# Dividing PSUM into three large and two small tiles in an encoder-layer kernel

## The chip, the cores and the metric

The kernel runs on one core of a Trainium2 chip. The metric is the device time of one execution in microseconds (us), taken as the median of several runs. Where a time is split up below, it comes from one profiled execution of the program.

## The reference

One layer of a bidirectional encoder is computed for two groups of tokens with the same weights: a group of 1024 tokens ("prompt") and one of 512 ("sample"), each with 256 memory tokens, at a model width of 1024, in float32. Cut to what matters:

```python
h = rms_norm(x, ln_pre)
z = h @ w_in            # 1024 -> 6400: inputs, gates and merge logits of all branches
pool_out  = multiscale_pool(pool_in, w_pool, pool_scale)     # 4 groups, windows 2, 4, 8, 16
attn_out  = self_attention(rope(norm(q)), rope(norm(k)), v)  # 8 heads of 64, 2 key heads
cross_out = cross_attention(xq, rms_norm(mem), w_mem_kv)     # 4 heads of 128, 256 memory tokens
branches  = pool_out * silu(pool_gate), attn_out * silu(attn_gate), cross_out * silu(x_gate)
merged    = sum(sigmoid(merge_logits[n] + b_merge[n]) * (branches[n] @ w_branch[n]) for n in range(3))
y         = x + rms_norm(merged @ w_out, ln_post)
```

## The kernel before

**Tiles.** Matrix products are made in parts: each operand is split into a high part and a low rest in the fp32r format (`split`, L164), and `mm3` (L132) adds three matmuls high x high, high x low and low x high in one PSUM sum. PSUM has eight banks of 512 float32 numbers in each of 128 partitions. Two helpers hand out all of it: `A()` (L91) gives a tile of 1024 numbers (two banks), of which there are two, and `B()` (L94) a tile of 512 (one bank), of which there are four. A tile that is asked for while all of its kind are in use is waited for: the first instruction that writes it waits for the last reader of the tile that had the place before. In SBUF there are, among others, eight half-wide buffers `HU()` (L85), three buffers `RAW()` for weights as loaded (L88), and two pairs for split weights (L168).

**Order of the work.** The program is written as Python generators that issue instructions stage by stage. The framework then orders the instructions of each engine by their place in the program, with some moved ahead (`tc.high_priority`, with EVAC = 200 for readers of PSUM) and by when the buffers that they need come free; so the order on each engine belongs to this program, and another division of buffers gives another order. Each engine runs its queue in order. All DMAs are issued from one queue, that of SyncE (SP).

**Stages.** (1) About 0 to 83 us: `mem_phase` (L660) makes keys and values of the memory tokens, and `long_h` (L232) normalises the group of 1024. It holds it as two by two blocks (features 0 to 511 and 512 to 1023 by tokens 0 to 511 and 512 to 1023). For each half of the tokens, `spread` (L209) brings the factors of the norm into a PSUM tile by a product with ones, and `scaled` (L254) multiplies the input by them.

(2) About 83 to 590 us: `products` (L318) makes the projections of the long group in pairs of 128 output channels. For each pair a two by two block product is made from seven block products in place of eight (Strassen's scheme in Winograd's form): the weights' sums are made on VectorE (L331 to L334), those of the input once in `long_h`. The seven products, 12 matmuls each, are added into three sums X, Y and Z in the order X Y X Z X Z X (L363), each in a B. Between them the sums are read: products 0, 2 and 3 are copied out by ScalarE (`keep`, L355 to L358), and products 1, 4 and 5 are added to such a copy by VectorE (`both`, L360, by `summed`, L416); the last is taken as it is. So X is read and written on four times, Z twice and Y once. There are 25 pairs. After each product a background task may run a step: the tails `kv_tail` (L567), `q_tail` (L595) and `pool_tail` (L622), which take an A for transposes (the first two) and Bs for small transposes or products.

(3) About 590 to 690 us: `plain` (L393) makes the first projections of the short group as ordinary products, 24 matmuls each into a B, with tails in the background (L1104).

(4) About 690 to 1150 us: attention. `stream` (L888) runs units of one head and 128 queries: `scores` (L771) makes scores in an A, takes the maximum (L782), the exponential (L784) and the division; `turn` (L789) transposes the result into another A and splits it (L165 and L162); `values` (L802) multiplies it with the values into a B that serves two units and is read by `gated` (L874, L882 and L883). `weave` (L108) puts between these the rest of the short group's projections (`plain` again, L1106), each in a B that L463 and L464 or L479 read. The cross-attention and the short group's attention follow in the same stream.

(5) From about 1150 us, for each of three blocks of 512 tokens: `branches` (L966) and `merge` (L981) make 24 merge products of 12 matmuls, each into a B that L996 multiplies with a loaded gate (`sg`, L988); then `out_phase` (L1003) makes the output in two halves. The first half uses two As (L1030, L1031), the second two Bs and an A. Their readers are L1026 and L1027; `finish` (L1011) makes the norm and the residual sum (L1020), and the store. In the last block the second half is cut up, with a further A (L1046) and `ending` (L1063).

Of the kernel before, what the change touches and what calls it, by code (L numbers as in the profile page):

```python
# [14 lines left out]
ALU = mybir.AluOpType  # L15
# [3 lines left out]
P = 128  # L19
D = 1024  # L20
KC = D // P
BLK = 512
# [39 lines left out]
def encoder_kernel(ctx: ExitStack, tc, wt, xs, xts, mt, cols, rows, rope, edge, ys):  # L62
    nc = tc.nc
    v, act, pool, pe = nc.vector, nc.scalar, nc.gpsimd, nc.tensor
# [4 lines left out]
    ps = ctx.enter_context(tc.tile_pool(name="ps", bufs=1, space=bass.MemoryType.PSUM))  # L69
# [5 lines left out]
    def nm(s):  # L75
        count[0] += 1
        return f"{s}_{count[0]}"
# [7 lines left out]
    def HU(dt=F32):  # L85
        return sb.tile([P, BLK], dt, tag="hu", bufs=NHU, name=nm("hu"))

    def RAW():  # L88
        return sb.tile([P, D], F32, tag="raw", bufs=NRAW, name=nm("raw"))

    def A(dt=F32):  # L91
        return ps.tile([P, 1024], dt, tag="A", bufs=2, name=nm("A"))

    def B(dt=F32):  # L94
        return ps.tile([P, 512], dt, tag="B", bufs=4, name=nm("B"))

    def S(n):
        return st.tile([P, n], F32, tag=f"s{n}", bufs=3 if n == 16 else 8, name=nm("s"))
# [5 lines left out]
    def run(g):  # L104
        for _ in g:
            pass
# [31 lines left out]
    def load(out, src):  # L138
        return nc.sync.dma_start(out, src)  # L139

    colt = const.tile([P, 44], F32, name="colt")
# [32 lines left out]
    def weights(*key, pieces=1):  # L174

        raw = RAW()
        load(raw[:], wt[TILES[key]])
        hi, lo = WT()
        with tc.high_priority(AHEAD):
            for i in range(pieces):  # L180
                s = slice(i * D // pieces, (i + 1) * D // pieces)
                split(hi[:, s], lo[:, s], raw[:, s])
        return lambda s: (hi[:, s], lo[:, s])
# [25 lines left out]
    def spread(r, out=None):  # L209

        dg = U()[:, :BLK]
        shape = [P, TT, P]
        v.tensor_tensor(dg.rearrange("p (t m) -> p t m", t=TT), ident[:].unsqueeze(1).broadcast_to(shape),
                        r.unsqueeze(2).broadcast_to(shape), op=ALU.mult)
        b = B()
        cost[0] += 3 * BLK / 2.4
        mm(b[:], ones[:], dg, start=True, stop=True)
        if out is None:
            return b[:]
        with tc.high_priority(EVAC):  # L220
            act.activation(out, b[:], AF.Copy)
# [10 lines left out]
    def long_h(xt, h):  # L232

        h += [[None] * 4 for _ in range(7)]
        xv = xt.rearrange("p (k t) -> p k t", k=KC)
        q = [[M(F32) for _ in range(2)] for _ in range(2)]
        for j in range(2):
            for i in range(2):
                load(q[i][j][:].rearrange("p (c n) -> p c n", c=4), xv[:, i * 4:i * 4 + 4, j * BLK:(j + 1) * BLK])
        yield  # L240
        r, sp, sq = S(16), [], []
        for j in range(2):
            sq.append([squares(q[i][j][:]) for i in range(2)])
            yield
        for j in range(2):
            rj = r[:, j * TT:(j + 1) * TT]
            mean_squares(sq[j], rj)
            rstd_of(rj)
            yield
            sp.append(spread(rj))  # L250
            yield
        b11, b12, b21, b22 = [[q[i][j][:, :D], q[i][j][:, D:]] for i in range(2) for j in range(2)]

        def scaled(i, j):  # L254
            for c in range(4):
                x = q[i][j][:, c * BLK:(c + 1) * BLK]
                v.scalar_tensor_tensor(x, x, colt[:, i * 4 + c:i * 4 + c + 1], sp[j], op0=ALU.mult, op1=ALU.mult)

        def put(k, x):
            for c in range(2):  # L260
                parts_of(h[k], 2 * c, x[c])

        def difference(out, a, b):
            for c in range(2):
                v.tensor_tensor(out[c], a[c], b[c], op=ALU.subtract)

        scaled(0, 0)
        put(0, b11)
        yield
        scaled(1, 0)  # L270
        put(1, b21)
        yield
        scaled(0, 1)
        scaled(1, 1)
        yield
        t3, t4 = (U(), U()), (U(), U())
        difference(t3, b22, b12)
        difference(b12, b12, b11)
        difference(b11, b22, b12)
        put(2, b11)  # L280
        put(3, b12)
        put(4, t3)
        put(5, b22)
        difference(t4, b21, b11)
        put(6, t4)
# [32 lines left out]
    def products(pairs, h, n, background):  # L318

        ops = {}  # L320

        def prepare():
            for p, (k0, k1, _) in enumerate(pairs):
                r0, r1 = RAW(), RAW()
                load(r0[:], wt[TILES[k0]])
                load(r1[:], wt[TILES[k1]])
                a11, a12, a21, a22 = r0[:, :BLK], r0[:, BLK:], r1[:, :BLK], r1[:, BLK:]
                ta, tb = SUM(), SUM()
                s2, s1, s3, s4 = ta[:, :BLK], ta[:, BLK:], tb[:, :BLK], tb[:, BLK:]
                with tc.high_priority(AHEAD):  # L330
                    v.tensor_tensor(s1, a21, a22, op=ALU.add)  # L331
                    v.tensor_tensor(s2, s1, a11, op=ALU.subtract)
                    v.tensor_tensor(s3, a11, a21, op=ALU.subtract)
                    v.tensor_tensor(s4, a12, s2, op=ALU.subtract)  # L334
                for i, x in enumerate((r0[:], ta[:], tb[:], a22)):
                    hi, lo = [w[:, :x.free_size()] for w in WT()]
                    with tc.high_priority(AHEAD):
                        split(hi, lo, x)
                    for k in range(2 if i < 3 else 1):
                        ops[p, 2 * i + k] = [w[:, k * BLK:(k + 1) * BLK] for w in (hi, lo)]  # L340
                    yield

        prep = prepare()
        done = 0

        def ready(i):
            nonlocal done
            while done < i and next(prep, prep) is not prep:
                done += 1

        for p, (_, _, take) in enumerate(pairs):
            banks = {}
            kept = {}

            def keep(k, b):  # L355
                kept[k] = HU()
                with tc.high_priority(EVAC):
                    act.activation(kept[k][:, :n], b, AF.Copy)  # L358

            def both(i, j, b, k):  # L360
                take(i, j, b, kept.pop(k)[:, :n])

            for i, bank in enumerate("XYXZXZX"):  # L363
                ready(p * 4 + i // 2 + LOOK)
                start = bank not in banks
                if start:
                    banks[bank] = B()
                b = banks[bank][:, :n]
                w = ops.pop((p, i))
                for c in range(4):  # L370
                    s = slice(c * P, (c + 1) * P)
                    mm3(b, (w[0][:, s], w[1][:, s]), h[i][c], start and c == 0, c == 3,
                        skip_group_check=True)
                    if c == 1:
                        yield
                if i == 0:
                    keep("p1", b)
                elif i == 1:
                    both(0, 0, b, "p1")
                elif i == 2:  # L380
                    keep("p16", b)
                elif i == 3:
                    keep("p5", b)
                elif i == 4:
                    both(1, 1, b, "p5")
                elif i == 5:
                    both(0, 1, b, "p16")
                else:
                    take(1, 0, b, None)
                next(background, None)  # L390
                yield

    def plain(pairs, h, background):  # L393

        for k0, k1, take in pairs:
            for i, key in enumerate((k0, k1)):
                w, b = weights(*key), B()
                for k in range(KC):
                    mm3(b[:], w(slice(k * P, (k + 1) * P)), h[k], k == 0, k == KC - 1)
                    if k == 3:  # L400
                        next(background, None)
                        yield
                take(i, 0, b[:], None)
                next(background, None)
                yield

    def summed(b, s, out=None):

# [682 lines left out]
    h, hs = [], []  # L1091
# [5 lines left out]
    sc, kt, vt, pairs, bg, tasks, drained = group(1)  # L1097
# [3 lines left out]
    run(drained(products(pairs[-4:], h, BLK, bg)))  # L1101
    run(pre)
    scs, kts, vts, pairs, bg, _, drained = group(0)
    run(plain(pairs[0], hs, bg))  # L1104
    merged = []
    fill = drained(plain(pairs[1], hs, bg))  # L1106
    units = [u for b in range(2) for u in attention(b, sc, kt, vt)]
    units += [u for b in range(2) for u in cross(b, sc, mkd[1], mvd[1])]
    units += pairs_of(scs, kts, vts) + cross(0, scs, mkd[0], mvd[0])
# [103 lines left out]
```

## Time and profile before

| | us |
|---|---|
| median of three runs | 1500.23 (1493.72 to 2429.65) |
| the profiled execution | 1496.65 |
| its span, first to last instruction | 1494.8 |
| TensorE busy with matmuls | 1456.0 |
| VectorE busy | 976.5 |
| ScalarE busy | 709.6 |
| GpSimd busy | 273.3 |
| mean granted clock of TensorE | 0.989 |

The profile names engines PE (TensorE; PEld is its loading of weights, which overlaps), DVE (VectorE), ACT (ScalarE), POOL (GpSimd) and SP (SyncE, whose queue issues the DMAs). A row of the time line has its start and length in us, the engine, the line of the kernel, the operation, the tiles as out<-in, shapes, the number of merged instructions, and in brackets the idle time before and what ended it. A row of a stretch has its length, then the busy time and the number of instructions of PE, PEld, DVE, ACT and POOL, the granted clock as a share of full speed, the share of DMA time and GB/s. A row of waits has who waited for whom, the us in total, how often, and the longest. The ends of matmuls are modelled, so that a matmul that starts 0.23 us after the one before it is shown as 0.39 us long; starts are the better guide. "whi" and "wlo" are split weights, "med" the split inputs, so that B<-med,whi is a product into a small tile.

### The profile page before, as it was taken

The numbers are of one execution on the slowest core, as the hardware profiler recorded it, in microseconds if no ns is written. First come the engines' busy times: TensorE is split into PE (matmuls) and PEld (weight loads), VectorE is DVE, ScalarE is ACT, GpSimd is POOL, SyncE is SP. The second block draws the span as 40 slices with busy tenths as digits, with TensorE's granted clock in tenths as the row PEclk, the third lists the DMA queues.
The fourth block names the chain that finished last, engine by engine and source line by source line (L and its number), as shares of the span: only waits on it lengthen the run. The fifth ranks groups of instructions, "written<-read, shape, count | busy, mean of one in ns | idle before, by whom it ended". The sixth has DMA issues, their size and how long they took to land.

```text
span 1494.8 us, 19564 instructions
## 1 busy us (share of the span) xinstructions
PE 1456.0 (97%) x7264; PEld 1210.1 (81%) x7264; DVE 976.5 (65%) x1215; ACT 709.6 (47%) x1083; POOL 273.3 (18%) x286
## 2 busy tenths in 40 slices
PE   7979999999999999999999999999998999999998
PEld 5768888888888888887888888888886888888887
DVE  6996586666648564747767666676775664764764
ACT  6444444544434545434656556566675233323332
POOL 1000020110000000301222222234232150250241
PEclk9989999999999999999999999999999999999999
DMA  7513233332422434344222223165446844954952
GB/s 277 172 47 106 85 114 125 108 132 66 129 92 78 158 133 128 102 150 148 64 96 80 91 68 106 58 219 173 155 155 214 286 148 132 347 193 140 336 163 84
DMA packets 88174, 211.37 MB, mean 141 GB/s; under 512 B 9872, under 2 KB 19216, under 8 KB 87312
## 3 DMA queue, kind: packets, MB, share of 16 engines
q1 hardware_dynamic: 88080, 210.14, 42.7%
q8 instruction: 57, 0.93, 0.3%
q14 instruction: 37, 0.30, 0.1%
HBM read 155.57 MB, written 54.53 MB: 141 GB/s over the span
## 4 chain that ended last, share of the span: by engine, by line
PE 85%; DMA 4%; DVE 4%; ACT 4%; issue 2%; SPq 1%; POOL 0%; DVEq 0%; POOLq 0%; ACTq 0%
PE B L126 66%; PE A L126 14%; PE A L130 5%; ACT u L784 1%; DVE s L782 1%; ACT whi L165 1%; DMA raw<-wt 1%; DVE wlo L162 1%; PE B L130 1%; DMA hu<-xq 1%; ACT med L165 1%; SPq L139 1%; DMA u<-x_prompt 0%; DMA hu<-merge 0%; DMA hu<-x_gate 0%
## 5 line engine op out<-in xcount | busy, mean ns | idle before, releaser
L126 PE MATMUL B<-med,whi 128*128 128x512 f32 x2776 | 871.2, 394 | 15.8 <-ACT med L165 15.8
L126 PEld LDWEIGHTS B<-med,whi 128*128 128x128 f32 x2776 | 515.8, 189 | 122.2 <-ACT med L165 17.5
L126 PE MATMUL B<-med,wlo 128*128 128x512 f32 x1388 | 544.1, 392 | 0.6 <-DVE wlo L162 0.6
L126 PEld LDWEIGHTS B<-med,wlo 128*128 128x128 f32 x1388 | 261.9, 189 | 56.6 <-DVE wlo L162 1.7
L162 DVE TENSOR_TENSOR wlo<-raw,whi 128x1024 fp32r<-128x1024 f32 (+1 forms) x169 | 213.3, 1263 | 141.6 <-ACT whi L165 140.7
L165 ACT ACTIVATE whi<-raw 128x1024 fp32r<-128x1024 f32 (+1 forms) x169 | 167.5, 991 | 288.5 <-PE B L126 198.3
L165 ACT ACTIVATE med<-A 128x1024 fp32r<-128x1024 f32 x92 | 94.3, 1025 | 108.4 <-PE A L130 108.2
L162 DVE TENSOR_TENSOR med<-A,med 128x1024 fp32r<-128x1024 f32 (+1 forms) x93 | 113.0, 1215 | 42.0 <-ACT med L165 40.8
L187 POOL TENSOR_SCALAR s<-s 128x16 f32<-128x16 f32 (+3 forms) x17 | 6.9, 404 | 669.0 <-DVE s L556 333.2
L786 POOL TENSOR_SCALAR u<-u,s 128x1024 f32<-128x1024 f32 x64 | 72.1, 1127 | 251.3 <-DVE s L785 219.1
L130 PE MATMUL A<-ident,u 128*128 128x128 f32 x784 | 102.8, 273 | 0.9 <-DVE med L162 0.2
L130 PEld LDWEIGHTS A<-ident,u 128*128 128x128 f32 x784 | 90.1, 140 | 16.3 <-issue 5.2
L998 POOL TENSOR_TENSOR med<-med,hu 128x512 f32<-128x512 f32 x48 | 77.0, 1617 | 142.3 <-DVE hu L996 142.2
L782 DVE TENSOR_REDUCE s<-A 128x1 f32<-128x1024 f32 x64 | 78.1, 1220 | 32.9 <-PE A L126 11.3
L126 PE MATMUL A<-kt,med 128*128 128x512 f32 x320 | 91.9, 409 | 2.7 <-ACT u L784 1.2
L126 PE MATMUL A<-whi,med 128*128 128x512 f32 (+1 forms) x320 | 92.4, 368 | 0.2 <-ACT hu L1027 0.2
L784 ACT ACTIVATE u<-A,s 128x1024 f32<-128x1024 f32 x64 | 71.3, 1114 | 38.4 <-DVE s L782 38.0
L165 ACT ACTIVATE whi<-sum 128x1024 fp32r<-128x1024 f32 x50 | 53.1, 1062 | 65.6 <-PE B L126 63.7
L162 DVE TENSOR_TENSOR med<-med,med 128x1024 fp32r<-128x1024 f32 (+1 forms) x50 | 55.8, 1127 | 38.1 <-ACT med L165 34.2
L165 ACT ACTIVATE med<-med 128x1024 fp32r<-128x1024 f32 (+1 forms) x44 | 44.2, 1017 | 74.8 <-POOL med L998 36.2
L162 DVE TENSOR_TENSOR wlo<-sum,whi 128x1024 fp32r<-128x1024 f32 x50 | 61.1, 1221 | 23.3 <-ACT whi L165 22.4
L126 PE MATMUL B<-med,vt 128*128 128x256 f32 x512 | 75.9, 287 | 0.4 <-ACT med L165 0.4
(179 smaller groups left out, 1610.4 us busy)
## 6 DMA issues: line engine op xcount, KB each, us to landing
raw<-wt SPq DMA_DIRECT2D x168, 512.0 KB, 3.7
merge<-hu SPq DMA_DIRECT2D x72, 256.0 KB, 2.0
hu<-merge SPq DMA_DIRECT2D x72, 256.0 KB, 5.2
med<-br SPq DMA_DIRECT2D x36, 256.0 KB, 5.6
q<-hu SPq DMA_DIRECT2D x24, 256.0 KB, 2.6
br<-hu SPq DMA_DIRECT2D x24, 256.0 KB, 2.3
med<-q SPq DMA_DIRECT2D x12, 512.0 KB, 5.0
med<-xt_prompt SPq DMA_DIRECT2D x4, 1024.0 KB, 13.2
```

Source lines behind the costliest of these rows:

```text
L126: pe.matmul(out, l, r, **k)
L130: pe.transpose(out, x, i[:])
L139: return nc.sync.dma_start(out, src)
L162: v.tensor_tensor(out, x, hi.bitcast(F32), op=ALU.subtract)
L165: act.activation(hi, x, AF.Copy)
L187: pool.tensor_scalar(ss, ss, EPS, 1.0, op0=ALU.add, op1=ALU.mult)
L782: v.reduce_max(mx[:], a[:], axis=AX.X, negate=True)
L784: act.activation(p, a[:], AF.Exp, bias=mx[:], accum_out=sm[:])
L786: pool.tensor_scalar(p, p, rc[:], 1.0, op0=ALU.mult, op1=ALU.mult)
L998: pool.tensor_tensor(at, at, sg[:], op=ALU.add)
```

## The change

There are three As and two Bs in place of two and four; both fill the eight banks. What used Bs beyond that is moved:

- In `products`, X and Z are the two halves of one A, which is asked for at the first product of a pair, and Y has a B.
- In `long_h`, the spread factors of the two halves of the tokens are copied by ScalarE from PSUM into a half-wide buffer each (by L221, which `spread` has for this already), and `scaled` reads them from there.
- `plain` is handed a function that gives it its sums: for the first projections of the short group the two of a pair are the halves of an A (`halves`); for those in the attention stage each has a B as before (`single`).

The merge products, the attention, the tails and the output phase are not edited; they draw on the new numbers of tiles. The diff:

```diff
--- before.py
+++ after.py
@@ -89,10 +89,10 @@
         return sb.tile([P, D], F32, tag="raw", bufs=NRAW, name=nm("raw"))
 
     def A(dt=F32):
-        return ps.tile([P, 1024], dt, tag="A", bufs=2, name=nm("A"))
+        return ps.tile([P, 1024], dt, tag="A", bufs=3, name=nm("A"))
 
     def B(dt=F32):
-        return ps.tile([P, 512], dt, tag="B", bufs=4, name=nm("B"))
+        return ps.tile([P, 512], dt, tag="B", bufs=2, name=nm("B"))
 
     def S(n):
         return st.tile([P, n], F32, tag=f"s{n}", bufs=3 if n == 16 else 8, name=nm("s"))
@@ -247,14 +247,15 @@
             mean_squares(sq[j], rj)
             rstd_of(rj)
             yield
-            sp.append(spread(rj))
+            sp.append(HU())
+            spread(rj, sp[j][:])
             yield
         b11, b12, b21, b22 = [[q[i][j][:, :D], q[i][j][:, D:]] for i in range(2) for j in range(2)]
 
         def scaled(i, j):
             for c in range(4):
                 x = q[i][j][:, c * BLK:(c + 1) * BLK]
-                v.scalar_tensor_tensor(x, x, colt[:, i * 4 + c:i * 4 + c + 1], sp[j], op0=ALU.mult, op1=ALU.mult)
+                v.scalar_tensor_tensor(x, x, colt[:, i * 4 + c:i * 4 + c + 1], sp[j][:], op0=ALU.mult, op1=ALU.mult)
 
         def put(k, x):
             for c in range(2):
@@ -363,9 +364,14 @@
             for i, bank in enumerate("XYXZXZX"):
                 ready(p * 4 + i // 2 + LOOK)
                 start = bank not in banks
-                if start:
-                    banks[bank] = B()
-                b = banks[bank][:, :n]
+                if bank == "Y":
+                    banks[bank] = B()[:, :n]
+                elif not banks:
+                    a = A()
+                    banks["X"] = a[:, :n]
+                elif start:
+                    banks[bank] = a[:, BLK:BLK + n]
+                b = banks[bank]
                 w = ops.pop((p, i))
                 for c in range(4):
                     s = slice(c * P, (c + 1) * P)
@@ -390,11 +396,11 @@
                 next(background, None)
                 yield
 
-    def plain(pairs, h, background):
+    def plain(pairs, h, background, bank):
 
         for k0, k1, take in pairs:
             for i, key in enumerate((k0, k1)):
-                w, b = weights(*key), B()
+                w, b = weights(*key), bank(i)
                 for k in range(KC):
                     mm3(b[:], w(slice(k * P, (k + 1) * P)), h[k], k == 0, k == KC - 1)
                     if k == 3:
@@ -403,6 +409,18 @@
                 take(i, 0, b[:], None)
                 next(background, None)
                 yield
+
+    def single(i):
+        return B()
+
+    def halves():
+        a = []
+
+        def bank(i):
+            if i == 0:
+                a[:] = [A()]
+            return a[0][:, i * BLK:(i + 1) * BLK]
+        return bank
 
     def summed(b, s, out=None):
 
@@ -1101,9 +1119,9 @@
     run(drained(products(pairs[-4:], h, BLK, bg)))
     run(pre)
     scs, kts, vts, pairs, bg, _, drained = group(0)
-    run(plain(pairs[0], hs, bg))
+    run(plain(pairs[0], hs, bg, halves()))
     merged = []
-    fill = drained(plain(pairs[1], hs, bg))
+    fill = drained(plain(pairs[1], hs, bg, single))
     units = [u for b in range(2) for u in attention(b, sc, kt, vt)]
     units += [u for b in range(2) for u in cross(b, sc, mkd[1], mvd[1])]
     units += pairs_of(scs, kts, vts) + cross(0, scs, mkd[0], mvd[0])
```

## The prediction

> **What bounds the kernel now.** I read the page's busy times first, then stretches of the run, then who waits for whom.
>
> ```profile
> span 1494.8 us, 19564 instructions
> PE 1456.0 (97%) x7264; PEld 1210.1 (81%) x7264; DVE 976.5 (65%) x1215; ACT 709.6 (47%) x1083; POOL 273.3 (18%) x286
> ```
> ```profile
> 83.40:680.00 596.60, 596.43 (x2731) 490.86 (x2732) 383.98 (x517) 267.61 (x380) 43.45 (x41) 0.99 0.35 111
> 692.00:1112.00 420.00, 415.78 (x2451) 351.92 (x2452) 288.36 (x356) 261.51 (x445) 126.08 (x145) 1.00 0.35 114
> ```
>
> TensorE is the bound. In the projections (83 to 680 us, where the block products run) it is idle for 0.2 us of 597; in the attention stage for 4.2 us of 420. The change leaves every product as it is, so it can win only idle time of TensorE: 1494.8 - 1456.0 = 38.8 us by the page, much of it at the start, where no PSUM tile is short. A faster result by 2% (30 us) is all but excluded. What can be lost is larger: 2 small tiles instead of 4 can stall an engine that is full.
>
> **Step 1, the third large tile: a gain in the attention stage.** Scores (L771 to L787) and transposes (L789 to L800) each take an A; with two, scores wait until the exponential of the scores before has been read out.
>
> ```profile
> PE A L126 <- ACT u L784: 1.4, 7, 0.4
> PE A L126 <- DVE med L162: 0.6, 1, 0.6
> ```
> ```profile
>   PEld A L126: 14.8, 39
> ```
> ```profile
> 976.44 1.11 ACT L784 ACTIVATE u<-A,s 128x1024 f32<-128x1024 f32 x1 [0.85 <-DVE s L782]
> ...
> 976.72 0.62 PE L126 MATMUL B<-med,whi 128*128 128x512 f32 x2
> ...
> 977.70 1.20 PE L126 MATMUL A<-kt,med 128*128 128x512 f32 x4 [0.35 <-ACT u L784]
> ```
> ```profile
> PE A L126 <- ACT hu L1027: 0.2, 1, 0.2
> ```
>
> The first two rows are waits of matmuls in 692 to 1112 us, 2.0 us in all. They understate it: the view counts 0.35 us at 977.70, but matmuls start 0.23 us apart (below) and the last of the pair at 976.72 starts near 976.95, so 0.5 us is lost. The row by itself, of who waits for readers and writers of A, has 39 waits of weight loads with 14.8 us; a load normally runs about a quarter of a microsecond ahead of its matmul, so 14.8 - 39 x 0.25 = 5 us reach TensorE. Bounds: 2.0 and 14.8. I take **-5 us**. The wait for L1027 to free the last A near the end (last row) goes too: **-0.2**.
>
> **Step 2, two small tiles at the block boundaries: a loss.** After a block's output phase the next block's merge products start, each 12 matmuls into a B, released by L996.
>
> ```profile
> 1267.74 0.62 PE L126 MATMUL B<-med,whi 128*128 128x512 f32 x2
> ...
> 1270.46 0.62 PE L126 MATMUL B<-med,whi 128*128 128x512 f32 x2
> ...
> 1273.18 0.62 PE L126 MATMUL B<-med,whi 128*128 128x512 f32 x2
> ```
> ```profile
> 1271.51 6.54 SPq L139 DMA_DIRECT2D hu<-merge  x10
> ...
> 1274.03 2.48 DVE L1020 SCALAR_TENSOR_TENSOR u<-med,s,u 128x1024 f32<-128x1024 f32 x2 [1.11 <-POOL s L191]
> 1276.42 1.88 DVE L996 SCALAR_TENSOR_TENSOR med<-hu,B 128x512 f32<-128x512 f32 x3
> ...
> 1279.49 0.50 PE L126 MATMUL B<-med,wlo 128*128 128x512 f32 x1 [0.25 <-DVE wlo L162]
> ```
> ```profile
> 1382.53 0.61 PE L126 MATMUL B<-med,whi 128*128 128x512 f32 x2
> ...
> 1385.76 2.02 DVE L996 SCALAR_TENSOR_TENSOR med<-hu,B 128x512 f32<-128x512 f32 x3
> ...
> 1388.96 0.50 PE L126 MATMUL B<-med,wlo 128*128 128x512 f32 x1 [0.38 <-DVE wlo L162]
> ```
>
> Products start at 1267.74, 1270.46 and 1273.18, 2.72 us apart (12 x 0.227). Their first release comes only at 1276.42: the gates that L996 reads are loaded from 1271.51 on, and VectorE finishes two L1020 before. Now four Bs bridge that. With two, the third product waits until the first L996 ends, 1276.42 + 0.68 = 1277.10 (0.68 is the mean of its row on the page's list): a stall of 1277.10 - 1273.18 = 3.9 us. At the second boundary the third product starts at 1382.53 and the release is 1385.76 + 0.68 = 1386.44: 3.9 us again. Queued behind the waiting matmul are all later products of the block; nothing else is left for TensorE there. The weight waits just after (0.25 and 0.38) vanish in the stall. Net 7.8 - 0.6 = **+7.2 us**. Bounds: 0, if the changed order brings gates and releases sooner, and 7.8.
>
> **Step 3, the clock after those stalls.**
>
> ```profile
> 72.44:75.85 3.41, 1.39 (x7) 0.81 (x5) 3.41 (x5) 1.39 (x2) 0.00 (x0) 1.00 1.04 294
> 75.85:89.50 13.65, 6.91 (x15) 5.08 (x16) 13.39 (x12) 6.50 (x8) 0.00 (x0) 0.50 0.02 6
> 1147.64:1151.05 3.41, 0.94 (x5) 0.43 (x3) 2.07 (x3) 0.00 (x0) 0.00 (x0) 1.00 0.93 356
> 1151.05:1155.62 4.57, 0.00 (x0) 0.00 (x0) 0.02 (x1) 1.06 (x1) 0.00 (x0) 0.50 0.94 289
> 1155.62:1161.29 5.67, 5.63 (x12) 3.93 (x13) 2.43 (x2) 1.06 (x1) 0.00 (x0) 0.50 1.01 369
> ```
>
> The granted clock is the column before the DMA share. It fell to 0.50 at 75.85 and 1151.05, 1075.2 us or 315 stretches of 3.41 us apart, as if it were decided once a stretch; in the stretch before each, TensorE was still busy for 1.39 and 0.94 us. So 2.0 us of idle time in one such stretch was enough, and a stall of 3.9 us puts at least 1.95 us into one of the two stretches that it touches. After the pause at 1151 the clock stayed at 0.50 for 5.67 us of work, which costs half of that, 2.8 us. Two boundaries: **+5.7 us**; bounds 0 and 9 (another stretch each). The Trainium skill (TensorE: Matmul & The Clock Gate, Part 1, "What's actually happening") has a free-running window of 3413 ns and a half clock after at least one idle window. The trace agrees on the window and not on the idle: by that rule a stall of 3.9 us seldom holds a whole idle window and the sum would lack these 5.7 us; I go by the row.
>
> **Step 4, two small tiles in the attention stage.** The value products keep a B until L883, the interleaved projections another until L464 or L479; now each has one.
>
> ```profile
> 757.42 1.20 PE L126 MATMUL A<-kt,med 128*128 128x512 f32 x4
> ...
> 757.89 0.69 DVE L464 SCALAR_TENSOR_TENSOR hu<-hu,B 128x512 f32<-128x512 f32 x1 [0.29 <-ACT hu L463]
> ...
> 759.25 1.19 PE L126 MATMUL B<-med,vt 128*128 128x256 f32 x8
> ...
> 760.27 0.63 PE L126 MATMUL B<-med,whi 128*128 128x512 f32 x2
> ...
> 762.24 0.42 DVE L883 TENSOR_TENSOR hu<-B,hu 64x256 f32<-64x256 f32 x1
> ...
> 764.74 1.19 PE L126 MATMUL B<-med,vt 128*128 128x256 f32 x8
> ...
> 830.08 1.19 PE L126 MATMUL B<-med,vt 128*128 128x256 f32 x8
> 830.17 0.41 DVE L883 TENSOR_TENSOR hu<-B,hu 64x256 f32<-64x256 f32 x1
> ```
>
> The projection's B is free at 758.58, its next product starts at 760.27; the values' B is free at 762.66, wanted at 764.74. The usual unit fits with 1.7 and 2.1 us to spare. Where no projection lies between two heads it doesn't: at 830.08 the next values start 0.5 us before L883 has ended. I count four such places (773, 830, 1046 and 1061), 0.5 to 1.2 us each and 3.7 in all; the order is made anew and can put a projection into some: **+2.5 us**. Bounds 0 and 18: the release takes 762.66 - 760.44 = 2.2 us after the values, scores and transposes alone cover 759.25 - 757.42 = 1.8, and 0.4 for each of 48 uses of L883 is 18.
>
> **Step 5, edits that I cost at nothing.** In the block products the sums X and Z become the two halves of an A, and Y alone stays in a B.
>
> ```profile
> L331 DVE TENSOR_TENSOR sum<-raw 128x512 f32<-128x512 f32 x25 | 17.3, 690 | 16.5 <-DMA raw<-wt 16.2
> ```
> ```profile
> L358 ACT ACTIVATE hu<-B x74: 577/598/602, 88.9 to 574.4; 128x512 f32<-128x512 f32 x74
> L416 DVE TENSOR_TENSOR hu<-B,hu x60: 678/692/693, 107.8 to 579.5; 128x512 f32<-128x512 f32 x60
> ```
> ```profile
> 32.76 0.60 ACT L221 ACTIVATE hu<-B 128x512 f32<-128x512 f32 x1 [2.08 <-PE B L126]
> ...
> 38.00 1.02 PE L126 MATMUL B<-u,ones 128*128 128x512 f32 x2
> ...
> 42.93 0.74 DVE L257 SCALAR_TENSOR_TENSOR med<-med,colt,B 128x512 f32<-128x512 f32 x1
> ```
>
> A half is read in 0.6 to 0.7 us while the other is written; the same sum returns two products, so 2.72 us, later. Y and the small transposes of the tails share two Bs at one use per 2.72 us. Cover gone, 25 pairs (L331) pay as the third rival says. The two new copies in the norm take 0.60 us each (the like one at 32.76) on an idle ScalarE; the first spread is done at 39.0, its first reader starts at 42.93. They hold two of eight half-wide buffers until about 69 us, so bounds are 0 and 1.4 (both copies and their handoffs); I take **0**, as VectorE, which that stage ends on, gets no more work. The halves for the short group's first projections have a third A for the tails: 0.
>
> **The sum** goes against the profiled execution: 1496.65 us, 1.85 beyond its span, and 0.24% below the shown median of 1500.23. 1496.65 - 5 - 0.2 + 7.2 + 5.7 + 2.5 + 0 = 1506.85: **1507 us**.
>
> **Rivals.** (1) The boundaries don't stall. Every queue's order is made anew with the program, and an earlier gate load or an L996 ahead of the two L1020 would release in time: 1496.65 - 5.2 + 2.5 = 1494. Against it: the gate loads stand behind weight loads and a store in the one SP queue, and none of these waits for a B. 25%. (2) The boundaries stall, but the clock stays: if a stretch had to be idle throughout, 3.9 us would rarely do it; 1507 - 5.7 = 1501. Against it stand the 1.39 and 0.94 busy us above. This is what the skill's sentence gives. 15%. (3) Slower, by one mechanism: the program guards an A as one object, so that a product into one half waits for the reader of the other. Place: the last four of the six changes of bank in a pair; price 2 x 0.6 + 2 x 0.69 = 2.6 us, x 25 = 64: 1571. It decides as soon as waits of TensorE for L358 and L416 appear in 83 to 590 us. For it: no row here shows a product writing one half while the other is read. Against it: the halves are separate banks of 512 numbers, and guarding by bank is enough by the Trainium skill (PSUM — Partial Sum Buffer, "PSUM bank collisions raise a hardware error"), which no run here tests. 7%. (4) The values starve at every head, step 4 at its upper bound: 1507 + 15.5 = 1522. Against it: the 2.1 us to spare. 10%. My forecast keeps 43%.
>
> **Range and chances.** 1488 to 1519: it reaches below (1) by the larger gain of step 1 and above the forecast by the upper bounds of steps 3 and 5 and most of step 4; (3), half of (4) and extremes stay out, under 2 in 10. A difference of 2% is about what a measurement of this kernel can tell from no change. Slower by more needs (3) or (4) with other losses: 0.09. Faster by more has no case but that the idle time at the start goes as well: 0.03. Within 2%: 0.88.
>
> **What would show it.** Right: after each of the two output phases, two merge products, a gap of about 4 us ended by L996, then a granted clock of 0.50 for some 5 us; in the attention stage no waits for L784 before scores; in the projections TensorE still idle for under 1 us. Wrong: the third merge product follows at once (steps 2 and 3 fall); waits for L784 stay (step 1); waits for L883 at many heads (4), or for L358 and L416 (5).

## The result and the profile after

The changed kernel takes 1618.56 us (median of 4 runs, 1617.17 to 1620.51), the kernel before 1498.28 beside it (median of 4). The ratio is 1.0815, with a 95% interval of 1.078 to 1.0849: slower. The ratio is taken over the fast runs alone, which leaves out a run of 2429.65 us of the kernel before. The prediction was 1507.

The busy times of the changed kernel, from its page:

```profile
span 1618.7 us, 19538 instructions
PE 1487.7 (92%) x7264; PEld 1212.6 (75%) x7264; DVE 978.9 (60%) x1215; ACT 713.6 (44%) x1085; POOL 271.8 (17%) x286
```

The work is the same: 7264 matmuls, and VectorE and ScalarE are busy nearly as long as before (978.9 us against 976.5, and 713.6 against 709.6). TensorE, which was idle for 3% of the span, is idle for 8%. Part of the lost time counts as busy: the last matmul before a wait is shown 0.39 us long, where its slot is 0.23. Where the loss lies is read by stages. I cut every trace at the same matmuls: the 49th matmul of the block products, the first matmul of `plain` for the first and for the later projections of the short group, and the first matmul of each block's merge products. Stretches of before and then of after between these points (length; busy time and count of PE, PEld, DVE, ACT, POOL; granted clock; DMA share; GB/s):

```profile
91.60:582.00 490.40, 490.23 (x2240) 403.69 (x2239) 322.25 (x429) 222.55 (x314) 29.07 (x28) 1.00 0.34 108
582.00:689.20 107.20, 107.20 (x511) 88.33 (x510) 62.34 (x95) 43.80 (x66) 14.38 (x13) 1.00 0.42 129
689.20:1155.60 466.40, 454.32 (x2687) 385.08 (x2685) 316.88 (x392) 289.54 (x507) 139.77 (x168) 1.00 0.38 124
```
```profile
92.40:676.60 584.20, 515.75 (x2238) 399.24 (x2239) 322.87 (x425) 221.44 (x312) 26.91 (x28) 1.00 0.28 91
676.60:802.80 126.20, 114.22 (x514) 90.85 (x513) 62.69 (x95) 43.68 (x66) 14.68 (x13) 0.96 0.38 118
802.80:1260.80 458.00, 449.05 (x2685) 388.96 (x2683) 314.76 (x392) 291.68 (x507) 140.16 (x168) 0.99 0.38 123
```

The first row of each is the block products: 490.4 us before, 584.2 after, with the clock at full speed in both. That is 93.8 of the 123.9 us by which the span grew. All stages, in us, from such cuts of each trace, with the experiments told below (each column with the start, up to the 49th matmul, adds up to the span):

| stage | before | after | h_xy | h_yz | s_sep | p_halves | g_single | n_late | m_three | d_attn3 |
|---|---|---|---|---|---|---|---|---|---|---|
| block products | 490.4 | 584.2 | 506.9 | 493.1 | 493.5 | 585.7 | 584.3 | 492.8 | 490.6 | 490.3 |
| short group's first projections | 107.2 | 126.2 | 125.6 | 125.4 | 125.7 | 124.8 | 116.5 | 116.7 | 107.3 | 108.9 |
| attention | 466.4 | 458.1 | 456.7 | 455.9 | 454.3 | 462.7 | 455.5 | 456.3 | 465.7 | 457.4 |
| merge and output, block 1 | 112.1 | 114.5 | 114.0 | 114.0 | 114.2 | 115.1 | 114.5 | 115.3 | 112.1 | 112.0 |
| block 2 | 109.3 | 119.0 | 117.4 | 118.9 | 120.1 | 109.4 | 117.8 | 117.7 | 110.3 | 109.4 |
| block 3 | 117.8 | 124.4 | 124.9 | 124.6 | 124.6 | 117.6 | 124.9 | 124.8 | 118.5 | 117.7 |

From before to after: +93.8, +19.0, -8.3, and +2.4 + 9.7 + 6.6 = +18.7.

Who keeps TensorE waiting in the block products of after, between 95 and 580 us (lines 358 and 416 of before are 359 and 434 here):

```profile
PE A L126 <- ACT hu L359: 24.1, 30, 1.0
PE A L126 <- DVE hu L434: 18.7, 26, 0.9
PE A L126 <- DVE u L434: 7.2, 9, 0.9
PE A L126 <- ACT whi L165: 5.8, 6, 1.0
```

These waits are 55.8 us, less than what is lost between 95 and 580 us, for the reason just given. The prediction named this view as what would show its third rival. Two changes of half in one pair, from the time line of after:

```profile
382.43 0.39 PE L126 MATMUL A<-med,wlo 128*128 128x512 f32 x1
382.92 0.69 DVE L434 TENSOR_TENSOR u<-A,hu 128x512 f32<-128x512 f32 x1 [2.94 <-PE A L126]
383.67 0.73 PE L126 MATMUL A<-med,whi 128*128 128x512 f32 x2 [0.85 <-DVE u L434]
...
386.29 0.39 PE L126 MATMUL A<-med,wlo 128*128 128x512 f32 x1
386.72 0.69 DVE L434 TENSOR_TENSOR u<-A,hu 128x512 f32<-128x512 f32 x1 [3.10 <-PE A L126]
...
387.46 0.72 PE L126 MATMUL A<-med,whi 128*128 128x512 f32 x2 [0.78 <-DVE u L434]
```

The last matmul of one product starts at 386.29, its reader at 386.72; the reader ends at 386.72 + 0.69 = 387.41 and the first matmul of the next product, which writes the other half, starts at 387.46. Back to back it would have started at 386.29 + 0.23. So 0.94 us are lost, and the same count gives 1.01 for the one above. The two changes ahead of these in that pair, behind L359, lose 0.85 and 1.14: 3.94 us in the pair. Over the stage, 93.8 / 25 is 3.75 us a pair.

The boundaries of the blocks, from the time line of after (L1014 is the merge's reader, L996 before; L1038 is L1020):

```profile
1380.02 5.69 SPq L139 DMA_DIRECT2D hu<-merge  x8
...
1380.56 0.39 PE L126 MATMUL B<-med,wlo 128*128 128x512 f32 x1
1381.63 2.48 DVE L1038 SCALAR_TENSOR_TENSOR u<-med,s,u 128x1024 f32<-128x1024 f32 x2 [1.10 <-POOL s L191]
1384.03 1.34 DVE L1014 SCALAR_TENSOR_TENSOR med<-hu,B 128x512 f32<-128x512 f32 x2
1384.86 1.19 PE L126 MATMUL B<-med,whi 128*128 128x512 f32 x2 [3.90 <-DVE med L1014]
```
```profile
1499.54 0.39 PE L126 MATMUL B<-med,wlo 128*128 128x512 f32 x1
...
1503.82 1.19 PE L126 MATMUL B<-med,whi 128*128 128x512 f32 x2 [3.90 <-DVE med L1014]
```

After two merge products nothing for 3.9 us, until the first L1014 is done, as worked out in the second step. The granted clock around both (stretches of 3.41 us):

```profile
1380.55:1383.96 3.41, 0.40 (x2) 0.00 (x0) 2.33 (x2) 1.06 (x1) 0.89 (x2) 1.00 0.95 338
1383.96:1387.37 3.41, 2.51 (x6) 2.06 (x7) 2.54 (x4) 0.00 (x0) 0.00 (x0) 0.50 1.04 392
1387.37:1390.79 3.42, 3.42 (x9) 2.65 (x9) 0.44 (x1) 0.00 (x0) 0.00 (x0) 0.50 0.84 310
1500.00:1503.41 3.41, 0.00 (x0) 0.00 (x0) 2.81 (x3) 0.84 (x1) 0.56 (x1) 1.00 1.02 347
1503.41:1506.83 3.42, 3.01 (x7) 2.46 (x8) 2.00 (x3) 0.00 (x0) 0.00 (x0) 0.50 1.04 401
1506.83:1510.24 3.41, 3.41 (x16) 2.77 (x16) 0.69 (x1) 0.00 (x0) 0.00 (x0) 1.00 0.74 248
```

The clock is the column of 1.00 and 0.50. It fell at 1383.96 and at 1503.41, and half of the busy time behind that is lost: (2.51 + 3.42) / 2 = 3.0 us and 3.01 / 2 = 1.5 us.

### The profile page after: what moved, and what is told of

It reads as the page before. It is cut to its first block, busy times and chain, and to the rows that moved or that the text cites. A ratio compares the mean times of both kernels' runs of the same rounds, so it can differ in the third digit from the quotient of the medians.

```text
span 1618.7 us, 19538 instructions
## 1 busy us (share of the span) xinstructions
PE 1487.7 (92%) x7264; PEld 1212.6 (75%) x7264; DVE 978.9 (60%) x1215; ACT 713.6 (44%) x1085; POOL 271.8 (17%) x286
## 4 chain that ended last, share of the span: by engine, by line
PE 43%; DVE 4%; DMA 3%; ACT 3%; issue 2%; POOL 1%; SPq 0%; DVEq 0%; POOLq 0%; ACTq 0%
PE B L126 26%; PE A L126 13%; PE A L130 4%; DMA med<-br 1%; ACT med L165 1%; DMA hu<-xq 1%; DVE wlo L162 1%; ACT whi L165 1%; POOL s L191 1%; DMA hu<-x_gate 1%; ACT u L949 0%; DVE med L162 0%; POOL med L1016 0%; DVE u L1038 0%; DVE s L945 0%
## 5 line engine op out<-in xcount | busy, mean ns | idle before, releaser
L126 PE MATMUL A<-med,whi 128*128 128x512 f32 x1488 | 477.7, 402 | 86.6 <-ACT hu L359 32.8
L126 PE MATMUL B<-med,whi 128*128 128x512 f32 x1288 | 408.3, 397 | 17.2 <-DVE med L1014 8.3
L126 PEld LDWEIGHTS A<-med,whi 128*128 128x128 f32 x1488 | 272.6, 190 | 179.0 <-ACT hu L359 50.5
L126 PEld LDWEIGHTS B<-med,whi 128*128 128x128 f32 x1288 | 241.3, 190 | 73.0 <-issue 10.7
L126 PE MATMUL A<-med,wlo 128*128 128x512 f32 x744 | 291.2, 393 | 0.0
L126 PE MATMUL B<-med,wlo 128*128 128x512 f32 x644 | 254.2, 395 | 0.0
L126 PEld LDWEIGHTS A<-med,wlo 128*128 128x128 f32 x744 | 140.8, 189 | 30.9
L126 PEld LDWEIGHTS B<-med,wlo 128*128 128x128 f32 x644 | 122.5, 190 | 26.1
L126 PE MATMUL A<-kt,med 128*128 128x512 f32 x320 | 88.3, 395 | 0.0
```

The costliest lines, as they stand in the source:

```text
L126: pe.matmul(out, l, r, **k)
```

## The experiments

The kernels h_xy, h_yz, g_single and d_attn3 ran beside a kernel before of 1493.66 us, the others beside one of 1494.04.

**h_xy: which sums share a tile.** The changed kernel with X and Y as the halves of the A and Z in a B:

```diff
-                if bank == "Y":
+                if bank == "Z" and start:
                     banks[bank] = B()[:, :n]
```

> The changed kernel with another pair of sums in the large tile: X and Y are its halves, Z has the small tile. Theory 1 (a large tile is guarded as one object, so a product into one half waits for the reader of the other half): of the four waits per pair in the changed kernel (0.85, 1.19, 1.0 and 0.95 us, 4.0 in all) only two remain, at the first change from X to Y and back, about 1.9 us per pair; the stage of the projections goes from 584 to about 535 us and the kernel from 1619 to about 1571 us. Theory 2 (the waits come from the number of tiles, a sum waiting for the place of an earlier tile): the numbers are the same and Z now presses on the two small tiles, so the stage stays at 584 us or grows.

Measured: 1541.1 us, ratio 1.0313 (1.0293 to 1.0334); the block products take 506.9 us. That is far from the alternative, but the expected size is missed by 30 us too: two waits a pair would be 50, and between 95 and 580 us only five waits for a reader of the A are on record, 4.9 us in all. The time line of the pair at 257 us shows how such a wait is covered:

```profile
257.70 0.39 PE L126 MATMUL B<-med,whi 128*128 128x512 f32 x1
257.93 0.39 PE L126 MATMUL B<-med,wlo 128*128 128x512 f32 x1
257.97 0.69 DVE L434 TENSOR_TENSOR u<-A,hu 128x512 f32<-128x512 f32 x1 [1.99 <-PE A L126]
258.15 0.61 PE L126 MATMUL B<-med,whi 128*128 128x512 f32 x2
...
258.72 0.73 PE L126 MATMUL A<-med,whi 128*128 128x512 f32 x2
```

The order was made anew: four matmuls into Z's B stand between the two products into the A, and L434 reads under them; about 0.1 us is lost (258.15 + 2 x 0.23 = 258.61 against 258.72). Such a product into another tile is a cover that the changed kernel doesn't have, since there only Y lies elsewhere and Y is done early.

**h_yz: sums that never alternate.** The same with Y and Z as the halves and X in a B:

```diff
-                if bank == "Y":
+                if bank == "X" and start:
                     banks[bank] = B()[:, :n]
-                elif not banks:
+                elif bank == "Y":
                     a = A()
-                    banks["X"] = a[:, :n]
+                    banks[bank] = a[:, :n]
```

> The changed kernel with Y and Z as the halves of the large tile and X in a small one. Y is read after the second product and Z is first written in the fourth, so no product into one half meets a reader of the other. Theory 1 (guarded as one object): all four waits go; the stage of the projections is back at 490 to 500 us and the kernel at 1525 to 1535 us. Theory 2 (number of tiles): X is the sum that is used most and takes one small tile nearly all the time, so waits grow; 584 us or more, kernel 1619 us or more.

Measured: 1525.02 us, ratio 1.0206 (1.0185 to 1.0226); block products 493.1 us. All waits of matmuls between 95 and 580 us:

```profile
PE B L126 <- ACT hu L359: 0.9, 2, 0.5
PE A L126 <- ACT hu L359: 0.9, 1, 0.9
```

With the same numbers of tiles and the same halves, only other sums in them, 91 of the 94 us are gone. The number of tiles is not the cause.

**s_sep: a bank for each sum as in the change, but not one tile.** Is it the program that guards the two halves together, or the chip that can't read one bank while its neighbour is written? In the stage of the block products PSUM is divided into one A, two Bs and four tiles `H()` of 512, and X and Z are Hs:

```diff
-                elif not banks:
-                    a = A()
-                    banks["X"] = a[:, :n]
                 elif start:
-                    banks[bank] = a[:, BLK:BLK + n]
+                    banks[bank] = H()[:, :n]
...
+    psum(1, 2, 4)
     run(products(pairs[:-4], h, BLK, bg))
...
     run(pre)
+    psum(3, 2, 0)
```

Here `psum` closes the PSUM pool and opens one with so many As, Bs and Hs.

> The changed kernel, in which X and Z of the block products are no longer halves of one tile but two tiles of 512 of their own kind: in that stage alone PSUM is one A, two Bs (for Y and the tails, as in the change) and four such tiles; all other stages keep the change's three As and two Bs. T1 (the program guards an A as one object, so that a product into one half waits for the reader of the other): the sums lie in banks as before, but no product waits for another sum's reader; the block products take 490 to 500 us (584 in the change, 490 before) and the kernel about 1618.6 - 89 = 1530 (1524 to 1536). T2 (it is the sharing of two Bs between Y and the tails, or a collision in the chip of one bank being read while its neighbour is written): both are still there, so the stage stays over 570 and the kernel over 1600.

Measured: 1521.8 us, ratio 1.0185 (1.0168 to 1.0202). The stage's row:

```profile
87.40:580.90 493.50, 490.63 (x2240) 403.56 (x2238) 324.18 (x430) 224.07 (x316) 28.28 (x28) 1.00 0.34 109
```

Between 95 and 580 us there is one wait for a reader of an H, of 0.6 us. Elsewhere TensorE writes one sum while the reader of the other runs; here it writes from 319.38 us on, and the reader ends at 319.29 + 0.69 = 319.98:

```profile
319.29 0.69 DVE L440 TENSOR_TENSOR hu<-H,hu 128x512 f32<-128x512 f32 x1 [2.39 <-PE H L135]
319.38 0.70 PE L135 MATMUL H<-med,whi 128*128 128x512 f32 x2
```

So it isn't the chip: the wait is put in by the program, which guards a tile as one object. The Trainium skill (PSUM — Partial Sum Buffer, "PSUM bank collisions raise a hardware error") says that guarding by bank is enough; these rows agree with it, and the coarser guard of the change costs 584.2 - 493.5 = 90.7 us here.

**p_halves: the halves alone.** All edits of the change with before's numbers:

```diff
-        return ps.tile([P, 1024], dt, tag="A", bufs=3, name=nm("A"))
+        return ps.tile([P, 1024], dt, tag="A", bufs=2, name=nm("A"))
...
-        return ps.tile([P, 512], dt, tag="B", bufs=2, name=nm("B"))
+        return ps.tile([P, 512], dt, tag="B", bufs=4, name=nm("B"))
```

> The change's edits (halves in the block products and in the first projections of the short group, copied spread factors) with the numbers of before, two As and four Bs. T1 (the halves alone bring the waits in the block products, 4.0 us a pair): block products 578 to 592 us, first short-group projections about 116 (107 and the 9.7 that single tiles gave back in the change), attention 466 and the three merge stages 112, 109 and 118 as before; the kernel 1494 + 94 + 9 = 1597 (1588 to 1605). T2 (the loss needs the scarce Bs as well): block products under 540. T3 (with two As the tails' transposes also fight with the sums for an A): block products over 600.

Measured: 1607.9 us, ratio 1.0766 (1.075 to 1.0782). The block products take 585.7 us, as in the change: halves alone bring all of that loss. Block 2 and 3 take 109.4 and 117.6 us as before: without the two Bs no boundary stalls. A miss is the stage of the short group's first projections: 124.8 us where 116 was expected. Waits of matmuls there, 680 to 804.5 us (first rows):

```profile
PE A L126 <- ACT med L432: 5.0, 4, 2.4
PE A L126 <- ACT whi L165: 2.2, 4, 0.9
PE A L130 <- ACT med L432: 1.5, 2, 1.3
```

L432 is the copy that reads a half. The halves cost 17.6 us in this stage, more than the 9.7 that g_single (next) took off the change. They do so with two As in place of three, and the last row is a wait of the tails' transposes for one of them; what the halves would cost with an A to spare was not run. The attention stage took 462.7 us (466 expected) and block 1 115.1 (112.1 before), which wasn't followed up.

**g_single: the short group's first projections back in Bs.** The changed kernel, one call altered:

```diff
-    run(plain(pairs[0], hs, bg, halves()))
+    run(plain(pairs[0], hs, bg, single))
```

> The changed kernel, with the first projections of the short group each in a small tile (as they were before) in place of halves of a large one. That stage is 126 us in the changed kernel and 107 before. Theory 1 (a large tile is guarded as one object): its nine waits of about 1 us between the halves go, and the large tiles are free for the tails, so 107 to 115 us, kernel 1600 to 1608 us. Theory 2 (number of tiles): with two small tiles shared with the tails' transposes the stage stays at 126 us or grows; kernel 1619 us or more.

Measured: 1607.51 us, ratio 1.0758 (1.0736 to 1.0779); the stage takes 116.5 us, a little over the 107 to 115 expected. With p_halves: the halves with two As and four Bs cost 17.6 us, two Bs shared with the tails 9.3 (116.5 - 107.2), and the change 19.0. The two costs don't add up; taking one away gives back only what the other doesn't hold.

**n_late: the numbers alone.** The kernel before, with three As and two Bs from the short group's first projections on and all its sums in Bs:

```diff
     run(pre)
+    psum(3, 2)
     scs, kts, vts, pairs, bg, _, drained = group(0)
```

> Before with three As and two Bs from the first projections of the short group on, all sums there in Bs; the stages ahead of it are as before. T1 (the numbers alone make the loss of the merge stages): block products 490, first short-group projections 116.5 (two Bs shared with the tails, as in the change with single tiles), attention 456 to 458, merge stages 114.5, 119 and 124.4 as in the change (112, 109 and 118 before), with gaps of about 4 us at the two block boundaries and a granted clock of 0.50 behind them; the kernel 1494 + 9 - 9 + 18.7 = 1513 (1508 to 1517). T2 (the merge stages lose because the block products before them put loads and buffers out of step): merge stages within 3 us of before in sum, the kernel at 1494 to 1498.

Measured: 1514.62 us, ratio 1.014 (1.0125 to 1.0155); 116.7 us in the first projections, 456.3 in the attention, 115.3 + 117.7 + 124.8 = 357.8 us in the merge stages against 339.2 before, +18.6. The boundaries (L1005 is the merge's reader here):

```profile
1276.41 0.39 PE L135 MATMUL B<-med,wlo 128*128 128x512 f32 x1
...
1280.71 0.88 PE L135 MATMUL B<-med,whi 128*128 128x512 f32 x2 [3.91 <-DVE med L1005]
```
```profile
1394.14 0.39 PE L135 MATMUL B<-med,wlo 128*128 128x512 f32 x1
...
1398.42 1.19 PE L135 MATMUL B<-med,whi 128*128 128x512 f32 x2 [3.89 <-DVE med L1005]
```

The same stalls as in the change, with block products as before ahead of them: the merge stages lose by the number of Bs and by nothing earlier. The time is 7.6 us above the prediction's, but it is made up otherwise: against before, +9.5 us in the first projections, -10.1 in the attention and +18.6 in the merge stages.

**m_three: one B more at the boundaries.** The kernel before, with two As and three Bs from the merge products on:

```diff
+    psum(2, 3)
     run(branches(0, sc, merged))
```

> Before with two As and three Bs (one bank unused) from the merge products on; all ahead of that as before. T1 (the boundary waits for the first L996, so each B more shortens the gap by a product of 2.72 us; the clock falls only after the long gap): gaps of 3.9 - 2.7 = 1.2 us at the two boundaries, the granted clock stays at 1.00 behind them, merge stages 112, 110.5 and 119; the kernel 2.4 us above before (1495 to 1498). T2 (the loss of 18.7 us in the merge stages is spread over many small waits for Bs and not tied to the boundaries' gaps and clock): merge stages 8 us or more above before in sum, the kernel at 1502 or more.

Measured: 1496.28 us, ratio 1.0013 (1.0004 to 1.0022); merge stages +1.7 us in all. First the two gaps, then the clock behind them:

```profile
1275.55 0.72 PE L135 MATMUL B<-med,whi 128*128 128x512 f32 x2 [1.09 <-DVE med L1005]
...
1385.83 0.74 PE L135 MATMUL B<-med,whi 128*128 128x512 f32 x2 [1.07 <-DVE med L1005]
```
```profile
1276.00:1282.00 6.00, 6.00 (x28) 4.94 (x27) 4.40 (x6) 1.06 (x1) 0.00 (x0) 1.00 1.01 368
1386.00:1392.00 6.00, 6.00 (x27) 4.92 (x28) 4.37 (x6) 1.06 (x1) 0.00 (x0) 1.00 1.01 364
```

The wait is for L1005 at both places, a product shorter, and the clock stays at 1.00. The third B is worth most of what four are worth here.

**d_attn3: the third A where it pays.** The kernel before, with three As and two Bs in the attention stage alone:

```diff
     run(plain(pairs[0], hs, bg))
+    psum(3, 2)
     merged = []
...
     run(fill)
+    psum(2, 4)
     run(branches(0, sc, merged))
```

> The kernel before, with PSUM divided anew by stage: two large and four small tiles everywhere, three large and two small in the attention stage alone; sums, copies and halves as in the kernel before. If the third large tile is worth what the changed kernel's attention stage shows (466.4 to 458.1 us): about 1498 - 8 = 1490 us, plus what the two new divisions cost at their borders (0 to 6 us). If the gain of that stage came from the stages around it, no gain: 1498 us or above. The projections stay at 490 us and the block boundaries show no 4 us gaps.

Measured: 1486.75 us, ratio 0.9945 (0.9928 to 0.9961): the fastest of all here, 6.9 us ahead of the kernel before; that is under 2%, but the interval lies clear of 1. The attention stage takes 457.4 us (466.4 before), the first projections 108.9 (107.2), and the other stages are as before. In 692 to 1112 us, the window whose waits for L784 the first step quoted, the waits of matmuls are now:

```profile
PE A L139 <- ACT u L940: 2.8, 1, 2.8
PE B L135 <- ACT med L174: 0.3, 1, 0.3
PE A L135 <- DMA med<-q: 0.3, 1, 0.3
```

No score waits for an exponential (L784 before, L793 here). Most of the gain of the change is there to be had without its losses, because a pool can be closed and another opened between stages.

## Why the prediction was wrong

**Step 5 failed.** It costed the halves in the block products at nothing, with the argument that "a half is read in 0.6 to 0.7 us while the other is written". In this program it is not: the third rival, which it gave 7%, is what happened. s_sep shows that the argument is right for the chip (493.5 us with separate tiles) and wrong for the guard (584.2 with one tile). The reason against the rival was a fact about banks; the question was about the program, and no row of before that I found shows a product writing one half of a tile while the other is read. That should have kept the chance higher than 7%.

The time line of before does show the guard, between two readers. In the output phase VectorE (L1026) and ScalarE (L1027) each read both halves of an A, and later two Bs:

```profile
1243.46 0.69 DVE L1026 TENSOR_TENSOR med<-A,u 128x512 f32<-128x512 f32 x1 [0.40 <-PE A L126]
...
1244.19 0.60 ACT L1027 ACTIVATE hu<-A 128x512 f32<-128x512 f32 x1 [2.38 <-DVE med L1026]
...
1244.91 0.69 DVE L1026 TENSOR_TENSOR med<-A,u 128x512 f32<-128x512 f32 x1 [0.75 <-ACT hu L1027]
...
1264.74 1.28 DVE L1026 TENSOR_TENSOR med<-B,u 128x512 f32<-128x512 f32 x2
```

On the A, VectorE's read of the second half (1244.91) waits 0.75 us until ScalarE has read the first, another bank. On two Bs its two reads follow one another without a wait (1264.74). So the program already guarded an A as one object.

**The rival's price was also too low**: 64 us, measured 93.8. Its place was right, the last four changes of bank in a pair. It took a wait to be as long as the reader, 0.60 or 0.69 us, and left out what stands on both sides of it. At 386.29 the last matmul starts; the reader starts 0.43 us later, 0.20 after that matmul's slot of 0.23 us, runs 0.69, and the next matmul starts 0.05 after it: 0.94. The losses of 0.85, 1.14, 1.01 and 0.94 us make 3.94 a pair where the price had 2.6.

**The short group's first projections** were part of step 5 too ("a third A for the tails: 0"). They lost 19.0 us: by the halves, or by two Bs shared with the tails, each enough for a good part (17.6 in p_halves, 9.3 in g_single). The longest wait in the change, 4.5 us before 700.38, is for L432, the reader of the sum just finished. It starts only at 699.75, behind a tail's step on ScalarE (L600), which waits for VectorE until 699.21.

**Steps 2 and 3 held.** Predicted 7.2 + 5.7 = 12.9 us; measured gaps of 1384.86 - 1380.56 - 0.23 = 4.07 and 4.05 us, and 3.0 + 1.5 by the clock, 12.6 in all. n_late, p_halves and m_three tie them to the number of Bs. The merge stages lost 18.7, though: the other 6 us are small waits, for L1014 and for split weights, that the steps did not list. Rivals 1 and 2, without the stall or without the slower clock, fall with this.

**Steps 1 and 4** were -5 and +2.5, together -2.5 us; the stage gained 8.3. Counted by the starts of matmuls, scores that wait for an exponential lost about 4.9 us before and none after, which is step 1's term. Values that wait for B's readers lose about 2.5 us after (1.2 for L482, 1.3 for L901), which is step 4's; so rival 4, up to 18 us, falls. (Its bound is 0.4 x 48 = 19; nothing hangs on the difference.) What the steps lacked: matmuls of scores without a wait on record also start sooner (about 4 us), a product of the cross-attention near the end waits 2.1 us for a B (L975, at 1254.22), and the pause at the end of the stage, 7.05 us before, shrank to 2.2 while 2.9 us appeared at another place (L949, at 1103.66). Why that pause moved was not tried; in p_halves, with two As, it is 5.0 us, so it doesn't hang on the third A alone.

**The copied spread factors** at 0 are not contradicted: the first product starts at 68.7 us after and at 68.2 before. They were not run alone.

**What luck there is.** Steps 1 to 4 came to +10.2 us, and the stages that they are about to -8.3 + 18.7 = +10.4. That agreement is luck: the attention gained 5.8 us more than forecast, and the merge stages lost 5.8 more (18.7 for 12.9). With none of step 5's halves (n_late) the time is 1514.62, within the range of 1488 to 1519, but there too by terms that partly cancel, with 9.5 us in the first projections, where its sums share two Bs with the tails, that no step had. With the block products mended alone (h_yz, s_sep) it is 1525.02 and 1521.8, still outside.

## What to carry to other kernels

Two sums that are written and read in turn should be two tiles, even where one large tile would cover the same banks: the program guards the whole tile, and each turn then costs the reader and its handing over, here 0.85 to 1.14 us. Sums that don't alternate can share one (h_yz). Before choosing one division of PSUM for a whole kernel, look at what each stage is short of; reopening the pool between stages gave the gain of the third large tile (9.0 us in its stage, 6.9 in the whole) without the price of two small ones at the block boundaries (18.6 us).

## What the runs showed of the hardware

- The clock fell after a stretch in which TensorE was busy for 0.40 us of 3.41 (1380.55 to 1383.96), so a wholly idle stretch isn't needed; 1.39 and 0.94 us before had shown the same. The two drops, at 1383.96 and 1503.41, lie 119.45 us or 35 such stretches apart. The Trainium skill (TensorE: Matmul & The Clock Gate, Part 1, "What's actually happening") asks for at least one idle window; only the stretch at 1500.00, with 0.00, agrees with that.
- It came back after a stretch with 3.01 busy us of 3.42 (1503.41 to 1506.83), and did not after one with 2.51 (1383.96 to 1387.37). A stall therefore cost 1.5 us or 3.0 by where it fell in the stretches, though both lasted 3.9.
- Gaps of 1.09 and 1.07 us in m_three left the clock at 1.00.
